# Second layer's modulations: all products on VectorE, and three of them made in the second layer itself

## The chip, the cores and the metric

The kernel runs on one core of one Trainium2 chip, as one launch. The metric is the device time of one execution in microseconds, the median of the runs; lower is better.

## The reference

Two layers of a hybrid backbone work on 128 context tokens and 512 latent tokens of width 1024, everything in fp32. Each layer has a mixing part (latent attention A, differential attention B, a Mamba-2 state-space part C, called SSD here, and one output projection) and a feed-forward part of width 4096. What the change touches are the modulations: six vectors per layer and per token group, made from the conditioning vector by one large weight matrix.

```python
mod = jax.nn.silu(c) @ w_ada[l] + b_ada[l]          # (6 * 1024); once for c_ctx, once for c
shift1, scale1, gate1, shift2, scale2, gate2 = jnp.split(mod, 6, axis=-1)
h = rmsnorm(x, p['norm1_g']) * (1.0 + scale1) + shift1
x = x + gate1 * mixing(h)
h = rmsnorm(x, p['norm2_g']) * (1.0 + scale2) + shift2
x = x + gate2 * (jnp.square(jax.nn.relu(h @ p['w_ff1'])) @ p['w_ff2'])
```

Modulation (l, j) below is vector j of layer l: j = 0 shift1, 1 scale1, 2 gate1, 3 shift2, 4 scale2, 5 gate2.

## The kernel before

All 640 tokens lie on the free axis, the features on the 128 partitions, in eight tiles. A matrix product takes each operand as two parts, a rounded one and the remainder, and adds three products of them on TensorE. ScalarE makes the rounded part of a weight tile (`wh`, line 1804 in the feed-forward part, line 296 in the mixing part) and VectorE subtracts it (`wl`, lines 1805 and 297). Weights come in 256 KB pieces over SyncE's DMA queue.

A layer runs as `mixing` and then `feed_forward`. `mixing` makes projections and SSD side by side, then attention B, then attention A, then the rest of the output projection (`wo`). `feed_forward` has four quarters q. In each, eight f1 units make 1024 hidden features (quarter 0 plainly, 1 to 3 in pairs, `ffx`, `ffy`, `ffz`), and eight f2 units multiply them by w_ff2 (`fm<-uh,wh`, line 1834). VectorE's `residual` (line 565) multiplies an f2 unit's result by the gate and adds it to `x`; until then the unit's PSUM tile is not free. The next layer's first norm is begun in the last quarter's f2 units.

The order on each engine comes from a scheduler, which takes the instructions as the code emits them. Work that has no fixed place is emitted in steps: a `Part` wraps a generator, and `weave` steps the part that is least far on by its own count. `pace(n)` sets the count of `fill`, the part of the modulations: n steps are spread over the part that is woven with it, and .01 means none. `FILL` holds the three values for projections with SSD, for the end of SSD, and for attention A.

Of the twelve modulations, (0,1) and (0,0) are made on TensorE at the start, (0,2), (0,3), (0,4) by `ada_dve` in the first layer's mixing part (the first by the end of SSD there, two in attention A), and the seven others by `ada_rows` in the first layer's feed-forward part. `ada_rows` spreads the two conditioning vectors over all partitions by 32 products with the identity (line 463, tiles `crow`), and then takes one step per 128 features: two DMAs of 256 KB (`wa`, line 470), and four products of 512 columns with their sum, one for each half of the inputs and each token group. `ROWS_POOL` says which two of the four go to GpSimd (a product at line 481, summed by ScalarE at line 482); the other two are one VectorE instruction each, product and sum (line 484). Eight steps make one modulation. In quarter 0 each f1 unit takes one step; each f2 unit takes two, save the first four of quarter 0.

The profile calls TensorE PE, VectorE DVE, ScalarE ACT, GpSimd POOL, SyncE SP.

Of the kernel before, what the change touches and what calls it, by code (L numbers as in the profile page):

```python
# [99 lines left out]
ADA_T = [(0, 5)] + [(1, j) for j in (1, 0, 2, 3, 4, 5)]  # L100
# [4 lines left out]
def build(nc, tc, a, ctx):  # L105
# [8 lines left out]
    def mark(s):  # L114
        if MARK:
            MARK(nc, s)
# [69 lines left out]
    def weave(need, *more):  # L186

        parts = list(need) + list(more)
        while any(p.live for p in need):
            e = min((p for p in parts if p.live), key=lambda p: (p.k + 0.5) / p.n)  # L190
            e.step()
# [255 lines left out]
    def ada_all(items):  # L447
        for l, j in items:
            for _ in ada_dve(l, j):
                mark("fill")  # L450
                yield
                mark("fill")

    def ada_rows(items):
# [19 lines left out]
        for i, (l, j, m, h) in enumerate(units):  # L474
            if m == 0 and h == 0:
                res = S([P, 2, KD, 2], "adares", 2)
            for v in range(2):
                junk = X([P, 512], name="junk")
                sum_ = res[:, h, m, v:v + 1]
                if 2 * h + v in ROWS_POOL:  # L480
                    pool.tensor_tensor(out=junk, in0=raws[i], in1=row[v][h], op=ALU.mult)  # L481
# [115 lines left out]
    def mixing(l, nrm, fill, late=None, raws={}):  # L597
# [1074 lines left out]
        def pace(n):  # L1672

            fill.k, fill.n = 0, n

        pace(FILL[0])
        ps_ssd, ps_proj = Part(ssd(), N_SSD, A_SSD), Part(projections(), N_PROJ)
        weave([ps_proj], ps_ssd, fill)
        p_b, p_pa = Part(att_b(), N_ATTB, A_ATTB), Part(prep_a(), N_PREP, A_PREP)
# [1 line left out]
        p_stack = Part(stack(), N_STACK, A_STACK)  # L1681
        while (0, 0, 2) not in stacks:
            p_stack.step()
        pace(FILL[1])
        weave([ps_ssd], p_b, p_pa, p_stack, fill)
        while l == 0 and fill.k < 9:
            fill.step()
# [3 lines left out]
        weave([p_b, p_pa, p_c], p_stack, fill)  # L1691
        p_s = Part(sub_all(sub_norm), N_SUB, A_SUB)
        p_a, p_w = Part(att_a(), N_ATTA, A_ATTA), Part(wo_part("wob", 4, range(2, 4), mixh, mixl, xsave, False), N_WO1)
        pace(FILL[2])
        weave([p_s], p_a, fill)
        weave([p_a, p_w], fill)
        while fill.live:
# [3 lines left out]
        for h in range(2):  # L1701
            for mi in range(4):
                mark(f"{l}wo")
                m = 4 * h + mi
# [17 lines left out]
    AHEAD = 1  # L1722
    FETCHED, AHEADS = 7, 2
    AP1, AP0 = (1, 4), ()
    FILL = (.01,6,25)
    ROWS_POOL = (1, 2)
    ADA_DVE = ((1, 4, 7), (1, 4, 7))
    CONV_POOL = ()
    ON_POOL = {f"xbc{j}" for j in range(2, 6)} | {"dv0", "dv1"}
# [144 lines left out]
    def feed_forward(l, nrm, fill):  # L1874
# [77 lines left out]
        for q in range(4):  # L1952
            uh, ul = [None] * 8, [None] * 8
            if q == 0:
                early(uh, ul)

                for m in range(8):
                    mark(f"{l}ff")
                    if m >= 2:
                        plain(m, uh, ul)  # L1960
                    fill.step()
            else:
                for m in range(4):
                    mark(f"{l}ff")
                    pair((m, m + 4), uh, ul)
                load_x(xsave, 0)
            for m in range(8):
                mark(f"{l}ff")
                if q and m + 1 < KD:
                    load_x(xsave, m + 1)  # L1970
                if q == 0 and m < 4:
                    next(expand)
                ps = PA("fm")
                for h in range(2):
                    block(halves(ps), W.next(), uh[4 * h:4 * h + 4], ul[4 * h:4 * h + 4], h == 0, h == 1)
                residual(l, 5, m, ps)
                nc.sync.dma_start(a["yT"][:, m] if l == DEPTH - 1 and q == 3 else xsave[:, m], x[m])
                if q == 3:
                    if l + 1 < DEPTH:
                        mark(f"{l + 1}norm1")  # L1980
                        nxt.scaled(l + 1, 0, m)
                        nxt.square(m)
                for _ in range(0 if q == 0 and m < 4 else 2):
                    fill.step()
        while fill.live:
            fill.step()
# [42 lines left out]
        act.copy(out=masksr[:, 0:4, :], in_=mk)  # L2029
        act.activation(out=never, in_=mk[:, M_SF:M_SB + 1], func=AF.Copy, scale=-1e30)  # L2030
    for l in range(DEPTH):
        f0 = Part(ada_all([(0, 2), (0, 3), (0, 4)]) if l == 0 else iter(()), 1)
        n2 = mixing(l, nrm, f0, *((second, raws0) if l == 0 else ()))
        f1 = Part(ada_rows(ADA_T) if l == 0 else iter(()), 57)
        nrm = feed_forward(l, n2, f1)


# [121 lines left out]
```

## Time and profile before

| | us |
|---|---|
| median of 3 runs | 1902.16 |
| lowest and highest of them | 1901.58, 1907.16 |
| the profiled execution | 1898.2 |
| its span, first to last instruction | 1896.4 |

The profile is of one execution, 4.0 us under the median of the runs and 1.8 us longer than its own span. Busy time counts work and leaves out waiting and issuing. In a row of a stretch each engine has its busy time in that stretch and the number of its instructions, then come the clock that TensorE was granted (1.00 is the upper of its two levels, 2.4 GHz, 0.50 the lower), the share of the DMA engines' time and GB/s. In a row of a group stand busy time and mean length in ns, then the idle time just before them and what ended it.

### The profile page before, as it was taken

How to read it: one execution, taken by the hardware profiler on the slowest of the kernel's cores; microseconds unless marked ns; L12 is line 12 of the kernel's file. 1: busy time of each engine (PE TensorE's matmuls, PEld its weight loads, DVE VectorE, ACT ScalarE, POOL GpSimd, SP SyncE). 2: the span in 40 equal slices, each digit the busy share in tenths (PEclk: the TensorE clock that was granted, in tenths of full speed). 3: DMA queues.
4: the chain of work that ended last, by engine and by line, in shares of the span. 5: the costliest groups of instructions: out<-in, count | busy, mean ns of one | idle time of the engine just before them, and what ended most of it. 6: DMA issues, size and time to landing. Idle time of an engine off the chain costs nothing. (4 is left out here: it accounts for less than half of the span.)

```text
span 1896.4 us, 31841 instructions
## 1 busy us (share of the span) xinstructions
PE 1735.2 (92%) x11508; PEld 1628.9 (86%) x11508; DVE 1432.1 (76%) x2587; ACT 915.3 (48%) x2009; POOL 797.5 (42%) x778
## 2 busy tenths in 40 slices
PE   6899985999898797997998899979998999999999
PEld 4798864888898797997998888768998999999999
DVE  7776778877979989889986775778746597565572
ACT  5543355665556454353555443266654454333240
POOL 4344345442546838648555443354303063130400
PEclk8899976989999999999999899879999999999999
DMA  9121123234253436456364221012121233534441
GB/s 333 48 84 41 48 61 99 66 122 137 84 167 116 135 125 213 163 188 210 99 203 132 59 63 54 23 53 77 62 73 45 73 115 93 165 109 141 126 150 57
DMA packets 116590, 209.02 MB, mean 110 GB/s; under 512 B 13392, under 2 KB 28624, under 8 KB 116432
## 3 DMA queue, kind: packets, MB, share of 16 engines
q1 hardware_dynamic: 115872, 206.80, 34.0%
q8 instruction: 91, 1.49, 0.3%
q14 instruction: 67, 0.55, 0.1%
q10 hardware_dynamic: 560, 0.18, 0.0%
HBM read 179.51 MB, written 27.43 MB: 109 GB/s over the span
## 5 line engine op out<-in xcount | busy, mean ns | idle before, releaser
L1834 PE MATMUL fm<-uh,wh 128*128 128x320 f32 x1024 | 239.2, 315 | 42.5 <-DVE x L565 42.5
L1804 ACT CAST wh<-wr 128x512 fp32r<-128x512 f32 x232 | 143.0, 617 | 221.2 <-PE fm L1834 134.0
L1805 DVE TENSOR_TENSOR wl<-wr,wh 128x512 fp32r<-128x512 f32 x232 | 204.0, 890 | 55.7 <-issue 38.9
L1834 PE MATMUL fm<-ul,wh 128*128 128x320 f32 x1024 | 238.6, 315 | 5.6 <-DVE ul L307 5.6
L481 POOL TENSOR_TENSOR junk<-wa,crow 128x512 f32<-128x512 f32 x112 | 186.9, 1689 | 126.1 <-DVE ul L307 31.9
L1834 PE MATMUL fm<-uh,wl 128*128 128x320 f32 x1024 | 237.2, 313 | 0.0
L1834 PEld LDWEIGHTS fm<-uh,wh 128*128 128x128 f32 x1024 | 174.6, 192 | 46.4 <-issue 31.9
L1834 PEld LDWEIGHTS fm<-ul,wh 128*128 128x128 f32 x1024 | 175.4, 192 | 7.2 <-DVE ul L307 7.2
L1834 PEld LDWEIGHTS fm<-uh,wl 128*128 128x128 f32 x1024 | 175.2, 192 | 0.0
L1791 POOL TENSOR_TENSOR wS<-wr,wr 128x512 f32<-128x512 f32 x48 | 76.4, 1591 | 168.3 <-DMA wr<-in_W 145.7
L484 DVE SCALAR_TENSOR_TENSOR junk<-wa,crow 128x512 f32<-128x512 f32 x112 | 139.1, 1271 | 9.0 <-DMA wa<-in_w_adaT 9.0
L565 DVE SCALAR_TENSOR_TENSOR x<-fm,mod,x 128x128 f32<-128x128 f32 (+2 forms) x192 | 72.3, 430 | 79.3 <-PE fm L1834 79.3
L785 PE MATMUL tm<-wl,hhi 128*128 128x256 f32 (+2 forms) x400 | 120.6, 302 | 4.2 <-POOL wl L297 4.2
L784 PE MATMUL tm<-wh,hhi 128*128 128x256 f32 (+2 forms) x400 | 121.5, 304 | 0.5 <-ACT xpad L628 0.5
L786 PE MATMUL tm<-wh,hlo 128*128 128x256 f32 (+2 forms) x400 | 120.3, 301 | 0.0
L482 ACT ACTIVATE junk<-junk 128x512 f32<-128x512 f32 x112 | 70.3, 628 | 89.2 <-POOL junk L481 89.2
L1804 ACT CAST wh<-wS 128x512 fp32r<-128x512 f32 x96 | 59.4, 621 | 108.0 <-PE fm L1834 37.3
L296 ACT CAST wh<-wr 128x512 fp32r<-128x512 f32 (+2 forms) x108 | 66.3, 624 | 72.8 <-PE fm L318 41.5
L1834 PE MATMUL ffx<-eh,wh 128*128 128x320 f32 x288 | 89.5, 311 | 3.1 <-ACT v L1935 3.0
L1834 PE MATMUL ffx<-eh,wl 128*128 128x320 f32 x288 | 88.8, 308 | 0.0
L1834 PE MATMUL ffx<-el,wh 128*128 128x320 f32 x288 | 88.8, 308 | 0.0
L785 PEld LDWEIGHTS tm<-wl,hhi 128*128 128x128 f32 x400 | 81.2, 203 | 5.0 <-POOL wl L297 4.5
(396 smaller groups left out, 5180.9 us busy)
## 6 DMA issues: line engine op xcount, KB each, us to landing
wr<-in_W SPq DMA_DIRECT2D x351, 256.0 KB, 2.8
wa<-in_w_adaT SPq DMA_DIRECT2D x112, 256.0 KB, 4.4
xsave<-x SPq DMA_DIRECT2D x72, 320.0 KB, 2.3
x<-xsave SPq DMA_DIRECT2D x72, 320.0 KB, 4.6
wa<-in_w_ada SPq DMA_DIRECT2D x48, 256.0 KB, 3.4
war<-in_w_ada SPq DMA_DIRECT2D x32, 256.0 KB, 5.5
x<-in_xT SPq DMA_DIRECT2D x16, 320.0 KB, 4.7
out_yT<-x SPq DMA_DIRECT2D x8, 320.0 KB, 2.2
```

The source lines that it names most:

```text
L296: act.copy(out=hi[:, :w], in_=raw[:, :w])
L481: pool.tensor_tensor(out=junk, in0=raws[i], in1=row[v][h], op=ALU.mult)
L482: act.activation(out=junk, in_=junk, func=AF.Copy, accum_out=sum_)
L484: vec.scalar_tensor_tensor(out=junk, in0=raws[i], scalar=1.0, in1=row[v][h], op0=ALU.mult, op1=ALU.mult, accum_out=sum_)
L565: vec.scalar_tensor_tensor(out=x[m][:, t0:t0 + n], in0=src, scalar=mods[l][:, j, m, v:v + 1], in1=x[m][:, t0:t0 + n], op0=ALU.mult, op1=AL ...
L784: pe.matmul(ps[:, i, :n], hh[k][:, ts], hi[:, c:c + n], start=s, stop=False)
L785: pe.matmul(ps[:, i, :n], hh[k][:, ts], lo[:, c:c + n], start=False, stop=False)
L786: pe.matmul(ps[:, i, :n], hl[k][:, ts], hi[:, c:c + n], start=False, stop=e)
L1791: pool.tensor_tensor(out=box[key], in0=box[x0], in1=box[x1], op=op)
L1804: act.copy(out=hi, in_=raw)
L1805: vec.tensor_tensor(out=lo, in0=raw, in1=f(hi), op=ALU.subtract)
L1834: mm = pe.matmul(o, w_, x_[:, ts], start=s_, stop=e_, skip_group_check=on)
```

## The change

Three things change. `ROWS_POOL` is empty, so that all four products of a step are VectorE's. The seven modulations of `ada_rows` are made in three places: (0,5), (1,1), (1,0), (1,2) in the first layer's feed-forward part, (1,3) and (1,4) in the second layer's mixing part, (1,5) in its feed-forward part; each place spreads the conditioning vectors anew. And an f2 unit takes one step instead of two, with `FILL` given per layer: for the second, 8 steps beside the projections and 9 beside attention A.

```diff
-        pace(FILL[0])
+        fills = FILL[l]
+        pace(fills[0])
...
-        pace(FILL[1])
+        pace(fills[1])
...
-        pace(FILL[2])
+        pace(fills[2])
...
-    FILL = (.01,6,25)
-    ROWS_POOL = (1, 2)
+    FILL = (.01, 6, 25), (8, .01, 9)
+    ROWS_POOL = ()
...
-                for _ in range(0 if q == 0 and m < 4 else 2):
+                if q or m >= 4:
                     fill.step()
...
-        f0 = Part(ada_all([(0, 2), (0, 3), (0, 4)]) if l == 0 else iter(()), 1)
+        f0 = Part(ada_all([(0, 2), (0, 3), (0, 4)]) if l == 0 else ada_rows([(1, 3), (1, 4)]), 1)
         n2 = mixing(l, nrm, f0, *((second, raws0) if l == 0 else ()))
-        f1 = Part(ada_rows(ADA_T) if l == 0 else iter(()), 57)
+        f1 = Part(ada_rows([(0, 5), (1, 1), (1, 0), (1, 2)] if l == 0 else [(1, 5)]), 57)
```

After the edit the lines from the first of these on stand one lower (line 1805 is 1806).

VectorE's order in the f2 units of quarter 1 of the first layer's feed-forward part, before (`junk` is a product that is summed, `x` the residual):

```order
L484 SCALAR_TENSOR_TENSOR junk_8157,adares_8051<-wa_8078,crow_6026 128x512
L484 SCALAR_TENSOR_TENSOR junk_8161,adares_8051<-wa_8152,crow_6023 128x512
L565 SCALAR_TENSOR_TENSOR x_7982<-fm_7986,mod_86,x_7982 128x128
L565 SCALAR_TENSOR_TENSOR x_7982<-fm_7986,mod_86,x_7982 128x192
L565 SCALAR_TENSOR_TENSOR x_7982<-fm_7986,mod_86,x_7982 128x320
L1805 TENSOR_TENSOR wl_8211<-wr_8113,wh_8210 128x512
L484 SCALAR_TENSOR_TENSOR junk_8171,adares_8051<-wa_8159,crow_6026 128x512
L484 SCALAR_TENSOR_TENSOR junk_8242,adares_8051<-wa_8166,crow_6023 128x512
L484 SCALAR_TENSOR_TENSOR junk_8252,adares_8051<-wa_8173,crow_6026 128x512
L484 SCALAR_TENSOR_TENSOR junk_8256,adares_8051<-wa_8247,crow_6023 128x512
L1805 TENSOR_TENSOR wl_8276<-wr_8178,wh_8275 128x512
```

Between the residuals of two f2 units stand four products and two remainders `wl`; the two `crow` tiles 6023 and 6026 are VectorE's. The same place after the change:

```order
L484 SCALAR_TENSOR_TENSOR junk_8127,adares_7042<-wa_8050,crow_6025 128x512
L484 SCALAR_TENSOR_TENSOR junk_8131,adares_7042<-wa_8056,crow_6024 128x512
L484 SCALAR_TENSOR_TENSOR junk_8133,adares_7042<-wa_8056,crow_6026 128x512
L484 SCALAR_TENSOR_TENSOR junk_8204,adares_7042<-wa_8129,crow_6023 128x512
L484 SCALAR_TENSOR_TENSOR junk_8206,adares_7042<-wa_8129,crow_6025 128x512
L565 SCALAR_TENSOR_TENSOR x_7898<-fm_7902,mod_86,x_7898 128x128
L565 SCALAR_TENSOR_TENSOR x_7898<-fm_7902,mod_86,x_7898 128x192
L565 SCALAR_TENSOR_TENSOR x_7898<-fm_7902,mod_86,x_7898 128x320
L1806 TENSOR_TENSOR wl_8094<-wr_8012,wh_8093 128x512
L484 SCALAR_TENSOR_TENSOR junk_8210,adares_7042<-wa_8135,crow_6024 128x512
L484 SCALAR_TENSOR_TENSOR junk_8212,adares_7042<-wa_8135,crow_6026 128x512
L484 SCALAR_TENSOR_TENSOR junk_8288,adares_8287<-wa_8208,crow_6023 128x512
```

Four products stand between one residual and the next in both; what is new is that the four `crow` tiles (6023 to 6026) are all VectorE's, and that an f2 unit makes one step, not two.

GpSimd's order at the same place before:

```order
L481 TENSOR_TENSOR junk_8054<-wa_7371,crow_6025 128x512
L481 TENSOR_TENSOR junk_8059<-wa_7378,crow_6024 128x512
L481 TENSOR_TENSOR junk_8068<-wa_8057,crow_6025 128x512
L481 TENSOR_TENSOR junk_8073<-wa_8064,crow_6024 128x512
L481 TENSOR_TENSOR junk_8149<-wa_8071,crow_6025 128x512
L481 TENSOR_TENSOR junk_8154<-wa_8078,crow_6024 128x512
L481 TENSOR_TENSOR junk_8163<-wa_8152,crow_6025 128x512
```

After the change no product is left on GpSimd; in these units it has nothing but the sums of weights `wS` for the pairs that come next.

VectorE's order in the second layer's mixing part, in the projections of dk, before (`dxn`, `dxr`, `dtmp` belong to the projections, `eg`, `xtm` to SSD):

```order
L758 TENSOR_TENSOR dxr_13017<-dxn_13007,tabs_11871 128x256 x2
L766 TENSOR_TENSOR dtmp_13018<-dxn_13007,tabs_11871 128x16x8 x2
L1183 TENSOR_TENSOR eg_13034<-eg_13034,dt_12257 128x512
L767 TENSOR_TENSOR dxr_13017<-dxr_13017,dtmp_13018 128x256
L1203 TENSOR_TENSOR xtm_12296<-yd_12971,xD_13068 128x512
L1185 TENSOR_TENSOR eg_13028<-eg_13028,eg_13034 128x512
L1186 TENSOR_TENSOR eg_13028<-eg_13028,cbm_12976 128x512
L297 TENSOR_TENSOR wl_13240<-wr_13237,wh_13239 128x512
L880 TENSOR_REDUCE ss_2863_13099<-dsq_13097 128x16
```

Nothing but projections, SSD and remainders of weights stands here. The same place after the change:

```order
L1186 TENSOR_TENSOR eg_12540<-eg_12540,cbm_12507 128x512
L881 TENSOR_SCALAR ss_2730_12665<-ss_2730_12665 128x16
L1183 TENSOR_TENSOR eg_12577<-eg_12577,dt_11842 128x512
L883 TENSOR_TENSOR dxn_12661<-dxn_12661,r_2731_12668 128x512
L758 TENSOR_TENSOR dxr_12671<-dxn_12661,tabs_11456 128x256 x2
L766 TENSOR_TENSOR dtmp_12672<-dxn_12661,tabs_11456 128x16x8 x2
L1185 TENSOR_TENSOR eg_12571<-eg_12571,eg_12577 128x512
L484 SCALAR_TENSOR_TENSOR junk_12693,adares_12024<-wa_12555,crow_11992 128x512
L484 SCALAR_TENSOR_TENSOR junk_12695,adares_12024<-wa_12555,crow_11994 128x512
L484 SCALAR_TENSOR_TENSOR junk_12699,adares_12024<-wa_12561,crow_11993 128x512
L484 SCALAR_TENSOR_TENSOR junk_12701,adares_12024<-wa_12561,crow_11995 128x512
L1183 TENSOR_TENSOR eg_12688<-eg_12688,dt_11842 128x512
```

The four products of a step stand between two instructions of SSD (`eg`). Nine such steps (36 products) lie beside the projections and SSD, seven (28) in attention A, eight (32) in the second layer's first f1 units, and 128 in the first layer's feed-forward part, 32 of them in its first f1 units.

## Rows read from the trace of the kernel before

**Rows 1.** The page: span, and busy time, share and instructions of each engine.
```profile
span 1896.4 us, 31841 instructions
...
PE 1735.2 (92%) x11508; PEld 1628.9 (86%) x11508; DVE 1432.1 (76%) x2587; ACT 915.3 (48%) x2009; POOL 797.5 (42%) x778
```

**Rows 2.** Stretches by engine: first layer's feed-forward (two), second layer's mixing and feed-forward.
```profile
core 0: us, PE busy (x) PEld busy (x) DVE busy (x) ACT busy (x) POOL busy (x), PEclk, DMA share, GB/s
513.40:578.60 65.20, 64.27 (x439) 63.33 (x438) 55.10 (x84) 40.07 (x94) 34.41 (x30) 1.00 0.46 147
578.60:1019.90 441.30, 389.43 (x2543) 382.50 (x2543) 408.26 (x589) 216.76 (x475) 283.35 (x183) 0.97 0.50 163
1020.20:1453.00 432.80, 397.97 (x2688) 357.03 (x2686) 303.30 (x664) 219.06 (x500) 165.30 (x217) 0.93 0.19 58
1453.00:1515.10 62.10, 61.52 (x406) 61.29 (x407) 33.71 (x46) 25.88 (x51) 4.92 (x3) 0.97 0.24 69
1515.10:1892.00 376.90, 374.94 (x2544) 374.07 (x2543) 230.59 (x356) 138.20 (x251) 90.78 (x64) 1.00 0.37 119
```

**Rows 3.** Waits of PE, 578.6 to 1019.9: who for whom, us, times, longest.
```profile
engine line waited for: us in total, times, longest us
PE fm L1834 <- DVE x L565: 40.5, 16, 6.9
PE fm L1834 <- DVE ul L307: 5.6, 6, 2.2
```

**Rows 4.** Waits of PE, 1515.1 to 1892, all of them.
```profile
PE fm L1834 <- DVE x L565: 2.0, 1, 2.0
```

**Rows 5.** Groups of DVE, 578.6 to 1019.9.
```profile
line engine op names shapes xcount | busy us, mean ns | idle before us <-releasers
L484 DVE SCALAR_TENSOR_TENSOR junk<-wa,crow 128x512 f32<-128x512 f32 x98 | 126.8, 1322 | 9.0 <-DMA wa<-in_w_adaT 9.0
L1805 DVE TENSOR_TENSOR wl<-wr,wh 128x512 fp32r<-128x512 f32 x96 | 96.4, 1019 | 4.9 <-issue 3.9 <-PE ffy L1834 1.1
...
L565 DVE SCALAR_TENSOR_TENSOR x<-fm,mod,x 128x128 f32<-128x128 f32 (+2 forms) x93 | 34.9, 427 | 2.5 <-PE fm L1834 2.5
...
L307 DVE TENSOR_TENSOR ul<-u,uh 128x640 fp32r<-128x640 f32 x26 | 28.7, 1105 | 0.5
```

**Rows 6.** Groups of DVE, 1515.1 to 1892.
```profile
L1805 DVE TENSOR_TENSOR wl<-wr,wh 128x512 fp32r<-128x512 f32 x96 | 71.6, 753 | 44.8 <-issue 32.5 <-PE ffy L1834 8.5 <-ACT wh L1804 2.2
...
L307 DVE TENSOR_TENSOR ul<-u,uh 128x640 fp32r<-128x640 f32 x25 | 21.5, 862 | 0.6
```

**Rows 7.** Timeline of DVE from 642: start us, us, instruction.
```profile
644.77 1.80 DVE L484 SCALAR_TENSOR_TENSOR junk<-wa,crow 128x512 f32<-128x512 f32 x1
...
646.50 0.68 DVE L484 SCALAR_TENSOR_TENSOR junk<-wa,crow 128x512 f32<-128x512 f32 x1
...
647.11 1.77 DVE L484 SCALAR_TENSOR_TENSOR junk<-wa,crow 128x512 f32<-128x512 f32 x1
```

**Rows 8.** Timeline of POOL, same stretch.
```profile
642.50 3.52 POOL L481 TENSOR_TENSOR junk<-wa,crow 128x512 f32<-128x512 f32 x2 [0.50 <-DMA wa<-in_w_adaT]
646.65 5.09 POOL L481 TENSOR_TENSOR junk<-wa,crow 128x512 f32<-128x512 f32 x3 [0.64 <-DVE junk L484]
```

**Rows 9.** Stretches as in rows 2: projections and SSD, then attention A, second layer.
```profile
1117.00:1210.00 93.00, 91.78 (x542) 73.31 (x542) 60.35 (x122) 35.26 (x86) 39.69 (x34) 0.93 0.18 53
1353.00:1449.00 96.00, 92.38 (x744) 90.33 (x744) 55.31 (x114) 51.76 (x113) 17.16 (x22) 1.00 0.17 55
```

**Rows 10.** The same, attention A of the first layer.
```profile
393.00:513.40 120.40, 109.53 (x812) 105.64 (x813) 92.83 (x197) 68.57 (x163) 45.02 (x46) 0.93 0.38 120
```

**Rows 11.** The products that spread the conditioning vectors: ns min/median/max, first and last start.
```profile
L463 PE MATMUL crow<-identr,sc x32: 270/275/275, 531.9 to 537.4; 128*128 128x128 f32 x32
```

**Rows 12.** The products, and the remainders of weights, on VectorE: ns min/median/max.
```profile
L484 DVE SCALAR_TENSOR_TENSOR junk<-wa,crow x112: 676/1747/1818, 542.1 to 1004.3; 128x512 f32<-128x512 f32 x112
L1805 DVE TENSOR_TENSOR wl<-wr,wh x232: 673/692/2012, 497.8 to 1874.5; 128x512 fp32r<-128x512 f32 x116
```

## The prediction, made before the changed kernel was run

> **What bounds the kernel now.** I read the page first. TensorE is busy for 92% of the span and VectorE for 76% [rows 1], so on average this is a TensorE kernel; but both layers do the same feed-forward work, and the average hides how they differ. So next I cut the span into stages [rows 2]. From the first f2 unit to the last, the second layer takes 376.9 us with TensorE busy for 374.9 of them. The first layer takes 441.3 us for the same products: TensorE is busy for 389.4, and VectorE for 408.3, 93% of the stretch. That is 64.4 us more, and the only work the first layer has on top is the modulations and the next layer's norm.
>
> Then the waits. In the second layer TensorE waits 2.0 us in that stretch [rows 4]. In the first it waits 40.5 us for residuals and 5.6 us for the remainder `ul` [rows 3], both VectorE's: an f2 unit cannot start because VectorE is late in emptying an earlier one's tile.
>
> Why VectorE is so late stands in its groups [rows 5]. The 98 products cost 126.8 us, 1322 ns each. Yet the shortest of the 112 takes 676 ns and the median 1747 [rows 12]: the instruction has two prices. The timeline tells them apart [rows 7, 8]. The product at 644.77 runs while GpSimd is in a product of its own and takes 1.80 us. The one at 646.50 starts in the gap of GpSimd that ends at 646.65 and takes 0.68; the next, at 647.11, falls into GpSimd's following run and takes 1.77. Other VectorE work with two inputs in SBUF pays too: 96 remainders `wl` take 1019 ns each here and 753 in the second layer, `ul` 1105 and 862 [rows 5, 6]. So the modulations cost VectorE twice, by its own products and by GpSimd's, which slow everything next to them.
>
> **The change, part by part.**
>
> *First layer, f2 units and pairs.* VectorE keeps its number of products in this stretch: 24 steps of four, 96, for 48 steps of two. What goes is GpSimd's share (and ScalarE's sums of it, which nobody on TensorE's path waits for). Per f2 unit with fill, VectorE has now three residuals (3 x 0.427), two remainders (2 x 1.019) and four products (4 x 1.322), 8.6 us [rows 5], against 48 products of TensorE at 376.9 / 2544 = 0.148 us, 7.1 us [rows 2]. So VectorE falls behind by 1.5 us in each of 24 units, 36 us; the rest of the 64 I put down to slower remainders elsewhere and to the lower clock (0.97 for 1.00). Without GpSimd the same unit has 1.28 + 2 x 0.753 + 4 x 0.68 = 5.5 us, and TensorE is the bound. For the whole stretch: VectorE's 230.6 us of the second layer, plus 96 products at 0.94 (GpSimd stays busy for 90.8 of 376.9 us there, a share of 0.24, with weight sums: 0.76 x 0.68 + 0.24 x 1.77), 90 us, plus some 20 us for norm and finishing, is 341 of 377. I leave 5 us for the norm in the last quarter and take 382 us: **-59**. Bounds: -64 if it becomes the second layer's; -20 if every product still costs 1.77 (170 + 231 + 20 = 421 us of VectorE, and the stretch as long as that).
>
> *First layer, f1 units.* 32 products replace 16, but 16 of GpSimd's go; VectorE is at 55.1 of 65.2 us with GpSimd busy for 34.4, and TensorE at 64.3 [rows 2]. **0**, between -1 and +5.
>
> *Spreading the vectors again, twice.* 32 small products on TensorE, started over 5.5 us among others [rows 11]; the first layer's f1 stretch, which has them, is 65.2 against 62.1 us [rows 2]. **+3** in each place (0 to 5.5).
>
> *Second layer, projections and SSD.* 36 products. TensorE is busy for 91.8 of 93 us, VectorE for 60.4, GpSimd for 39.7, a share of 0.43 [rows 9]. At 0.57 x 0.68 + 0.43 x 1.77 = 1.15 us they are 41 us, and VectorE has 33 idle. They also stand in the queue ahead of SSD's `eg`, which TensorE will want. Most is covered by the projections, which need little of VectorE; what is not covered shows at the end of SSD. I take **+12**, between 0 (all in idle time) and +41 (all on the path), nearer the first, since TensorE has no idle time to give there. The 16 steps' DMAs, two of 256 KB each, join SyncE's queue among the weights; the DMA engines are busy for 0.18 of this stretch, so I cost them at nothing; without that cover a weight would come later by a step's two transfers.
>
> *Second layer, attention A.* 28 products. VectorE is busy for 55.3 of 96 us, GpSimd for 17.2, a share of 0.18 [rows 9]: 28 x (0.82 x 0.68 + 0.18 x 1.77) = 25 us into 41 idle. But softmax chains run through VectorE. The first layer makes two modulations in this same stage and takes 120.4 us [rows 10], 12.2 more per modulation, with TensorE work and GpSimd sums that the new form does not have. 28 products are 7/8 of a modulation: at most 10.7 by that row. **+8**, between 0 and +25.
>
> *Second layer, f1 units.* 32 products at 0.68, 22 us, into 28 idle us of VectorE (33.7 of 62.1 busy, GpSimd 4.9 [rows 2]): **0** beside the spreading, up to +8.
>
> Sum: -59 + 0 + 3 + 12 + 8 + 3 = **-33 us** against the profiled execution's 1898.2, which gives 1865. The median of the runs is 4.0 us above that execution, so 1902.2 - 33 = **1869 us**.
>
> **A rule that speaks against it.** An undisturbed product with its sum takes 0.68 us [rows 7], no more than a remainder of the same size, which makes no sum: 692 ns in the median [rows 12]. The Trainium skill, "Vector Engine (DVE) Microarchitecture Reference", section "Points that are easy to get wrong", says that this form with two fp32 inputs from SBUF runs at half throughput, since both read ports are taken. No row of this trace shows such a halving where GpSimd rests, so I give it little, as the fourth rival. By that rule an undisturbed product would be an estimated 1.38 us, twice a remainder, and the outcome that rival's.
>
> **The rivals.**
>
> 1. *The second layer hides it all* (TensorE is full there, VectorE has idle time): -59 + 3 + 3 = -53, 1849 us. Against it: SSD and softmax wait in VectorE's queue. 15%.
>
> 2. *VectorE becomes the bound of the projections: slower.* The 36 products meet SSD's own GpSimd work and cost 1.77 each, 64 us, all ahead of `eg`; attention A pays 10.7. -59 + 3 + 64 + 11 + 3 = +22, 1924 us. It decides once the second layer pays more than 59 us, that is more than 53 for 64 products, 0.83 us each on the path. For it: 41 us of products for 33 idle. Against: GpSimd is busy for only 0.43 of it [rows 9]. 4%.
>
> 3. *The first layer stays VectorE's* because the weight sums and the norm's sums on GpSimd fall on the products: -20 + 26 = +6, 1908 us, on the edge of no difference. Against: the second layer has the same weight sums and its remainders cost 753 ns [rows 6]. 5%.
>
> 4. *The products are dear in themselves*, and 1322 ns is their own price. The stretch keeps 127 us of products and loses only the slower remainders, 25 + 7 us [rows 5, 6]: 376 busy, at today's 93% 406 us, -35. The second layer's 20 us become 20 x 1322 / 1000 = 26, and its f1 units want 33.7 + 42 of 62 us, +14; the first's +5. -35 + 3 + 26 + 14 + 3 + 5 = +16, 1918 us. 2%.
>
> That the change does not do what it says is excluded by the order of the instructions: 224 products, all on VectorE.
>
> **How the numbers follow.** The forecast has 74%, the rivals 15, 4, 5 and 2. Its own terms reach from about -52 (half of each cost in the second layer) to -15 (first layer -50, projections +20, attention A +10), so the range is 1850 to 1887 us; it leaves out half of the first rival and the last three. About 0.3%, 5.7 us, is what a measurement of this kernel can tell from no change. Faster: 74 + 15, 0.89. Same: most of the third rival, 0.04. Slower: the second, the fourth and what is left of the third, 0.07.
>
> **What would show it right or wrong.** In the profile of the changed kernel the first layer's f2 stretch should last about 382 us, with VectorE near 340 and TensorE's wait for residuals under 10; products should have a mean near 0.8 us there, and `wl` near 0.75. The second layer's mixing part, 432.8 us now, should be near 456, its f1 stretch near 65. The prediction is wrong if the first layer's stretch stays above 400, or if the mixing part grows by over 40; in the latter case the wait to look for is TensorE's for `eg` or for the attention parts behind SSD.

## The result, and the profile after

The changed kernel takes 1879.2 us, the median of 4 runs (1877.8 to 1880.3), against 1901.9 for the kernel before in the same series: a ratio of 0.989, 95% interval 0.986 to 0.991. The forecast was 1869 us, range 1850 to 1887. The profiled execution takes 1878.6 us, its span is 1876.8, 19.6 below the span before [rows 1].

The page after, span and busy time by engine:

```profile
span 1876.8 us, 31813 instructions
...
PE 1744.0 (93%) x11572; PEld 1641.7 (87%) x11572; DVE 1387.1 (74%) x2811; ACT 851.1 (45%) x1793; POOL 606.2 (32%) x666
```

GpSimd lost 191 us of work and VectorE 45, though VectorE now makes twice as many products. The stages after, in the order of [rows 2]: first layer's f1 units, its f2 units and pairs, the second layer's mixing part, f1 units, f2 units and pairs.

```profile
516.50:580.40 63.90, 63.54 (x437) 63.02 (x436) 50.52 (x108) 31.44 (x64) 7.63 (x13) 1.00 0.49 153
580.40:974.00 393.60, 379.05 (x2547) 377.34 (x2546) 309.61 (x587) 154.45 (x279) 115.14 (x85) 0.99 0.46 150
974.30:1423.30 449.00, 410.45 (x2717) 367.51 (x2716) 346.89 (x796) 222.15 (x505) 166.69 (x217) 0.90 0.24 74
1423.30:1486.70 63.40, 63.40 (x437) 63.40 (x438) 47.69 (x102) 28.03 (x55) 4.50 (x3) 1.00 0.45 137
1486.70:1872.00 385.30, 378.27 (x2545) 376.84 (x2544) 230.48 (x369) 138.17 (x251) 93.95 (x64) 0.99 0.37 117
```

Against [rows 2] these are -1.3, -47.7, +16.2, +1.3 and +8.4 us, together -23.1; the first layer's mixing part, which is the same program in both, and the ends make up the other 3.5. So the first layer wins nearly 48 us and the second gives 26 back, 8 of them in its f2 units, beside which no step is emitted.

TensorE's waits in the first layer's f2 stretch after (us, times, longest), where it waited 46 us in all [rows 3]:

```profile
PE fm L1835 <- DVE x L565: 8.0, 4, 4.3
PE fm L1835 <- DVE ul L307: 6.5, 3, 3.7
```

VectorE's groups in the same stretch, those of [rows 5]:

```profile
L1806 DVE TENSOR_TENSOR wl<-wr,wh 128x512 fp32r<-128x512 f32 x96 | 75.4, 796 | 18.3 <-issue 12.2 <-PE ffy L1835 4.0 <-ACT un L1901 1.2
L484 DVE SCALAR_TENSOR_TENSOR junk<-wa,crow 128x512 f32<-128x512 f32 x101 | 73.4, 776 | 1.8 <-DMA wa<-in_w_adaT 1.7
```

The same number of products (101 for 98) costs 73.4 us instead of 126.8, and a remainder `wl` takes 796 ns instead of 1019. This is the step on which the forecast rested, and it is there as forecast.

Quarter 0's eight f2 units, first layer before, second layer before, first after, second after, as stretches of their own, each up to the first product of the pairs:

```profile
578.60:653.40 74.80, 59.73 (x385) 58.27 (x384) 74.50 (x106) 40.19 (x86) 58.05 (x37) 0.95 0.38 120
1515.10:1574.90 59.80, 57.85 (x384) 57.59 (x384) 48.78 (x72) 28.39 (x53) 34.60 (x26) 0.97 0.35 110
```
```profile
580.40:653.50 73.10, 61.40 (x385) 60.21 (x385) 63.73 (x117) 28.96 (x53) 34.97 (x24) 0.93 0.34 108
1486.70:1554.80 68.10, 61.07 (x385) 60.34 (x385) 52.09 (x85) 28.56 (x53) 40.80 (x27) 0.92 0.30 96
```

Nearly the whole 8.4 us of the second layer's f2 stretch are in its quarter 0 (68.1 for 59.8). The first layer's quarter 0 is still 13 us above 59.8, and hardly shorter than before the change (73.1 for 74.8): nearly all of the 47.7 us were won behind it. In the second layer's quarter 0 TensorE now waits 7.0 us where it waited 2.0 [rows 4], and it is busy for 3.2 us more at a granted clock of 0.92 for 0.97. Its waits in the second layer's f2 stretch after:

```profile
PE fm L1835 <- DVE ul L307: 3.7, 1, 3.7
PE fm L1835 <- DVE x L565: 3.3, 1, 3.3
```

What happens there shows at the end of the second layer's f1 units. VectorE's timeline after (start, us, instruction):

```profile
1491.07 0.82 DVE L1894 SCALAR_TENSOR_TENSOR u<-un 128x640 f32<-128x640 f32 x1
1491.81 0.69 DVE L484 SCALAR_TENSOR_TENSOR junk<-wa,crow 128x512 f32<-128x512 f32 x1
...
1493.64 0.69 DVE L484 SCALAR_TENSOR_TENSOR junk<-wa,crow 128x512 f32<-128x512 f32 x1
...
1494.26 1.94 DVE L1849 SCALAR_TENSOR_TENSOR nh<-x,amul,nR 128x128 f32<-128x128 f32 x4
1496.11 0.82 DVE L307 TENSOR_TENSOR ul<-u,uh 128x640 fp32r<-128x640 f32 x1
```

The same `ul` before the change:

```profile
1520.43 0.82 DVE L307 TENSOR_TENSOR ul<-u,uh 128x640 fp32r<-128x640 f32 x1
```

The last f1 unit's `u` is ready at 1491.9, but its remainder `ul`, which the f2 units need, stands behind four products and the first instructions (`nh`, line 1849) of the expansion, which makes from the norm's result the operands of the pairs. It ends at 1496.9, 10.2 us after the stretch began. Before the change the first `nh` stand ahead of it too, and it ends 6.2 us after the stretch began: the products make it 4 us later.

Two theories come out of this. The first: what GpSimd's products took from VectorE was the cost, and the move to the second layer was needed as well, since an f2 unit with eight products would be 1.28 + 1.5 + 8 x 0.69 = 8.3 us of VectorE for TensorE's 7.1. Its rival: GpSimd was all of it, and the move only costs. The second theory: the 8 us in the second layer's quarter 0 come from the products of (1,5) in its f1 units.

### The profile page after: what moved, and what is told of

Its sections match the earlier page's. It is cut to its first block, busy times and chain, and to the rows that moved or that the text cites. A ratio compares the mean times of both kernels' runs of the same rounds, so it can differ in the third digit from the quotient of the medians.

```text
span 1876.8 us, 31813 instructions
## 1 busy us (share of the span) xinstructions
PE 1744.0 (93%) x11572; PEld 1641.7 (87%) x11572; DVE 1387.1 (74%) x2811; ACT 851.1 (45%) x1793; POOL 606.2 (32%) x666
## 5 line engine op out<-in xcount | busy, mean ns | idle before, releaser
L1835 PE MATMUL fm<-ul,wh 128*128 128x320 f32 x1024 | 237.0, 313 | 10.2 <-DVE ul L307 10.2
L1806 DVE TENSOR_TENSOR wl<-wr,wh 128x512 fp32r<-128x512 f32 x232 | 179.7, 782 | 80.8 <-issue 48.5
L1835 PE MATMUL fm<-uh,wl 128*128 128x320 f32 x1024 | 235.9, 312 | 0.0
L1792 POOL TENSOR_TENSOR wS<-wr,wr 128x512 f32<-128x512 f32 x48 | 72.4, 1509 | 329.3 <-DMA wr<-in_W 281.5
L484 DVE SCALAR_TENSOR_TENSOR junk<-wa,crow 128x512 f32<-128x512 f32 x224 | 156.4, 747 | 5.0 <-DMA wa<-in_w_adaT 4.8
L1805 ACT CAST wh<-wS 128x512 fp32r<-128x512 f32 x96 | 59.8, 623 | 147.0 <-PE fm L1835 70.7
L784 PEld LDWEIGHTS tm<-wh,hhi 128*128 128x128 f32 x400 | 82.3, 206 | 5.2 <-DVE zth L805 2.8
L1806 DVE TENSOR_TENSOR wl<-wS,wh 128x512 fp32r<-128x512 f32 x96 | 76.8, 800 | 11.5 <-issue 11.0
```

Source lines behind the costliest of these rows:

```text
L484: vec.scalar_tensor_tensor(out=junk, in0=raws[i], scalar=1.0, in1=row[v][h], op0=ALU.mult, op1=ALU.mult, accum_out=sum_)
L784: pe.matmul(ps[:, i, :n], hh[k][:, ts], hi[:, c:c + n], start=s, stop=False)
L1792: pool.tensor_tensor(out=box[key], in0=box[x0], in1=box[x1], op=op)
L1805: act.copy(out=hi, in_=raw)
L1806: vec.tensor_tensor(out=lo, in0=raw, in1=f(hi), op=ALU.subtract)
L1835: mm = pe.matmul(o, w_, x_[:, ts], start=s_, stop=e_, skip_group_check=on)
```

## Experiments

### One half of the change each

GpSimd's products alone, from the kernel before:

```diff
-    ROWS_POOL = (1, 2)
+    ROWS_POOL = ()
```

> The kernel before, with all four products of a step on VectorE; two steps per f2 unit and all seven modulations in the first layer stay. Theory (GpSimd's products slow VectorE's two-input work, and an f2 unit is late when VectorE's work between two residuals exceeds TensorE's 7.1 us): a unit has 1.28 + 1.5 + 8 x 0.69 = 8.3 us of VectorE for 7.1, against 8.6 before, so the first layer's f2 stretch stays VectorE's and falls only from 441 to between 415 and 435 us; time 1877 to 1895. Rival A (all of the gain is from taking GpSimd off): the stretch falls to about 394 as in the changed kernel, and with nothing in the second layer the time is about 1853. Rival B (products cost 1.3 us of their own): stretch above 480, time above 1940.

The move alone, from the changed kernel:

```diff
-    ROWS_POOL = ()
+    ROWS_POOL = (1, 2)
```

> The changed kernel, with two of a step's four products on GpSimd as before. Theory (what counts is VectorE's work per f2 unit): one step leaves 1.28 + 2 x 1.0 + 2 x 1.32 = 5.9 us for TensorE's 7.1, so the first layer's f2 stretch is within 10 us of the changed kernel's 393.6, and the second layer pays some more in its mixing part (449 to 465), where GpSimd has work of its own: time 1880 to 1900. Rival (taking GpSimd off is what gave the first layer its gain): the stretch stays above 415, time above 1905.

GpSimd's products alone give 1863.4 us, ratio 0.982 (0.980 to 0.984): 16 us faster than the changed kernel. The move alone gives 1898.5, ratio 0.999 (0.996 to 1.002): nothing. First layer's f2 stretch and second layer's mixing part, of the first half alone (e1) and then of the move alone (e2):

```profile
579.50:984.80 405.30, 383.53 (x2547) 379.46 (x2547) 380.83 (x787) 153.99 (x280) 120.80 (x85) 0.98 0.55 176
985.00:1418.40 433.40, 397.93 (x2686) 358.52 (x2684) 300.99 (x664) 218.72 (x500) 167.00 (x217) 0.93 0.19 58
```
```profile
577.30:987.50 410.20, 384.67 (x2547) 381.44 (x2546) 318.71 (x485) 186.67 (x379) 196.67 (x135) 0.97 0.45 144
987.80:1442.90 455.10, 409.43 (x2717) 364.77 (x2715) 343.25 (x732) 241.02 (x569) 207.41 (x249) 0.91 0.24 73
```

The kernel before, the changed one and these two make a square. The f2 stretch is 441.3 us before, 405.3 without GpSimd's products, 410.2 with the move alone, 393.6 with both. Each half by itself brings most of the gain there, but only the move has a price in the second layer: once GpSimd is out, it buys 11.7 us in this stretch and costs 25 in the second layer. Of e1's expectations none came: the stretch lies between the theory's (415 to 435) and rival A's (394), and the time, 1863, is nearer to rival A's 1853 than to the theory's 1877; rival B is far off. The theory's error is in 0.69 us a product: that is how long its record lasts, but in the queue the next begins before the record ends, 0.61 us after the start of the one before (1491.81 to 1493.64 above is three steps). Over the stretch VectorE's 380.8 us fit into 405.3. Of e2 the theory's time (up to 1900) and mixing part came, but the stretch is 16.6 us above the changed kernel's, where 10 were allowed; the rival asked for over 415 and over 1905. So the sum of an f2 unit (5.9 us for 7.1) is not all. TensorE still waits 20.6 us for residuals in e2's stretch, 10.8 of them in quarter 0 and 9.8 early in the f2 units of quarters 1 and 2, where VectorE comes to a run of products at up to 1.77 us each.

### What GpSimd's operation does to VectorE

On the kernel of e1, useless work for GpSimd that nobody waits for: once a product that reads a `crow` tile twice, once fills (`jk` is a tile of its own).

```diff
+        jk = Y([P, 512], name="jk")
...
+            pool.tensor_tensor(out=jk, in0=row[1][h], in1=row[1][h], op=ALU.mult)
```

> The kernel of e1 (all seven modulations in the first layer, all products on VectorE), and two products on GpSimd per step whose result nobody uses: both inputs are spreading tiles in SBUF, the output is a tile of its own, no engine waits for it. GpSimd so does as much as in the kernel before (112 products of 1.69 us), while VectorE has nothing less to do. Theory (two inputs from SBUF on VectorE and a GpSimd operation that reads SBUF exclude each other): products beside them take 1.77 us again, their mean in the first layer is above 1.1 us, the f2 stretch grows from 405 to between 455 and 500 us and the time from 1863 to between 1913 and 1960. Rival (GpSimd's results, ScalarE's sums of them and the waits for them were what cost, not GpSimd's reading): stretch within 8 us of 405.

```diff
+        jk = Y([P, 512], name="jk")
...
+            for _ in range(4):
+                pool.memset(jk, 0.0)
```

> The kernel of e1, and on GpSimd four fills of a 128x512 tile in place of each useless product of e5: GpSimd is as busy to within a third or so, but reads nothing. Theory (reading is what excludes): products stay at 0.69 us, f2 stretch within 5 us of 405, time 1858 to 1868. Rival (any GpSimd operation on SBUF slows VectorE): products with a mean above 1.0 us, the stretch above 440.

With the reads 1936.8 us, ratio 1.020 (1.016 to 1.024); with the fills 1864.6, ratio 0.982 (0.978 to 0.986), the time of e1. VectorE's products and GpSimd's useless work over the whole program, reads (e5) and then fills (e6):

```profile
L485 DVE SCALAR_TENSOR_TENSOR junk<-wa,crow 128x512 f32<-128x512 f32 x224 | 205.4, 960 | 0.0
...
L487 POOL TENSOR_TENSOR jk<-crow 128x512 f32<-128x512 f32 x112 | 158.8, 1418 | 17.6 <-ACT bsh L559 9.4 <-ACT crow L464 1.4
```
```profile
L485 DVE SCALAR_TENSOR_TENSOR junk<-wa,crow 128x512 f32<-128x512 f32 x224 | 163.3, 773 | 0.0
...
L488 POOL MEMSET jk<- 128x512 f32 x448 | 235.9, 527 | 22.5
```

The fills keep GpSimd busy for longer (235.9 us for 158.8) and cost nothing: products have 773 ns, in e1 772, the first layer's f2 stretch takes 405.7 us for 405.3, and all that the theory expected came. The reads lengthen products to 960 ns. The first layer's f1 and f2 stretches with the reads:

```profile
518.10:601.60 83.50, 68.10 (x438) 66.13 (x437) 74.78 (x103) 30.40 (x64) 58.21 (x51) 0.94 0.35 108
601.60:1061.30 459.70, 395.85 (x2548) 388.70 (x2547) 442.99 (x795) 154.07 (x282) 228.26 (x162) 0.96 0.49 157
```

They are 18 and 54 us longer than e1's; 73 us for 112 GpSimd products, 0.65 us each on TensorE's path. The theory's times and its stretch came; its mean for a product (above 1.1 us) did not, since the useless products also ran beside other work of VectorE: in the f2 stretch a remainder `wl` has 904 ns with the reads and 775 with the fills. The residuals, whose one input lies in PSUM, have 425 and 426 ns. This is what the Trainium skill, "SBUF — State Buffer", section "Who interferes with whom", states: a VectorE instruction with two inputs from SBUF gets in the way of a GpSimd instruction that reads SBUF, not of one that only writes it. These two runs agree with it; a GpSimd operation with one input was not tried.

### The products left out

From the changed kernel, once without the products of the mixing part, once without those of the second layer's f1 units; their sums are set to zero (shown for the first; the second has `((1, 5),)` there):

```diff
+                skip = (l, j) in ((1, 3), (1, 4))
...
-                if 2 * h + v in ROWS_POOL:
+                if skip:
+                    pass
+                elif 2 * h + v in ROWS_POOL:
```

> The changed kernel without the 64 products of (1,3) and (1,4); their DMAs, the spreading of the vectors and the finishing stay. Theory (the products' place in VectorE's queue is what the mixing part pays): its 449.0 us fall to 433 to 437, time 1863 to 1868. Rival (spreading, DMAs on SyncE's queue and TensorE's clock are what it pays): the part stays above 443.

> The changed kernel without the 32 products of (1,5) in the second layer's f1 units; DMAs, spreading and finishing stay. Theory (these products push VectorE's work into quarter 0's first f2 units, where the expansion of the norm's result already fills it): the f2 stretch falls from 385.3 to 376 to 379 us and the f1 stretch from 63.4 to 62 to 63.4; time 1868 to 1873. Rival (the 8 us in the f2 stretch are of another origin, such as a transfer or the clock): the stretch stays above 383.

Without the mixing part's products: 1854.0 us, ratio 0.977 (0.975 to 0.980). The part takes 428.5 us, 20.5 less than with them and 4 less than before the change. So spreading the vectors and the DMAs cost nothing there that these runs can tell; the price is the products'. The part's own data don't depend on (1,3) and (1,4), which the feed-forward part uses. Both numbers are better than the theory's 433 to 437 and 1863 to 1868; how far mixing parts of nearly one program differ from run to run is told below. Without the products of (1,5): 1872.3 us, ratio 0.986 (0.983 to 0.989). The second layer's f1 and f2 stretches:

```profile
1423.70:1488.60 64.90, 64.90 (x437) 64.90 (x438) 33.39 (x48) 27.51 (x55) 4.48 (x3) 0.97 0.43 134
1488.60:1865.80 377.20, 375.33 (x2545) 374.43 (x2544) 228.50 (x356) 138.21 (x251) 91.36 (x64) 1.00 0.38 119
```

The f2 stretch is back at 377.2 us, as before the change (376.9): the second theory holds, its rival falls. The f1 stretch is 2.8 us above that of before, which leaves the spreading; its expectation (62 to 63.4) did not come.

How the mixing part pays shows in its 30 us slices at the end of SSD, at the same distance from the part's start. Changed kernel, then the one without the products:

```profile
1154.00:1184.00 30.00, 27.60 (x137) 21.26 (x136) 23.82 (x47) 7.37 (x20) 6.95 (x6) 0.73 0.24 71
1184.00:1214.00 30.00, 23.20 (x110) 18.89 (x109) 25.97 (x63) 10.89 (x25) 6.11 (x8) 0.67 0.20 63
1214.00:1244.00 30.00, 24.36 (x104) 17.96 (x104) 21.51 (x61) 21.93 (x55) 16.76 (x39) 0.69 0.18 55
```
```profile
1150.00:1180.00 30.00, 29.86 (x161) 24.01 (x160) 24.72 (x47) 8.24 (x20) 7.42 (x7) 0.79 0.30 89
1180.00:1210.00 30.00, 22.16 (x134) 19.15 (x133) 20.47 (x58) 20.89 (x50) 10.77 (x26) 0.89 0.20 60
1210.00:1240.00 30.00, 25.33 (x156) 21.09 (x157) 25.16 (x69) 22.08 (x57) 19.39 (x31) 0.89 0.16 54
```

With the products TensorE does 351 matmuls in 90 us, without them 451, at a granted clock of 0.67 to 0.73 instead of 0.79 to 0.89. Over the whole part TensorE is idle for 5.6 us more (38.5 for 32.9) and busy for 14.9 more, at a clock of 0.90 for 0.94: three quarters of the 20.5 us are TensorE's own work, more of it at the lower level. The fall of the clock goes with the waits; that they cause it was not tried by itself. Which of VectorE's results came late first is not settled; the trace names only single waits there.

### Better places

On e1, quarter 0's expansion in f2 units 0, 2, 4, 6, no steps in that quarter's f2 units. In both kernels the expansions from the second on read x after a residual has been added, so their values differ, not their instructions.

```diff
-                if q == 0 and m < 4:
+                if q == 0 and m % 2 == 0:
                     next(expand)
...
-                for _ in range(0 if q == 0 and m < 4 else 2):
+                for _ in range(2 if q else 0):
```

> The kernel of e1, with the expansion of the norm's result put into quarter 0's f2 units 0, 2, 4, 6 instead of 0, 1, 2, 3, in both layers, and no steps in quarter 0's f2 units (the others take two each, which makes the same 56 steps). Theory (quarter 0 is late because VectorE has f1's backlog, the expansion and steps at once): quarter 0's eight units take some 65 us in the first layer for 79, and 58 for 61 in the second; f2 stretches 390 to 399 and 372 to 376, time 1848 to 1858. Rival (VectorE is full over the whole stretch, 381 of 405 us, so that what quarter 0 saves comes back in quarter 3, which now has eight more steps): first layer's stretch above 402, time 1858 to 1865.

Then also a step beside each pair (the loop above becomes `range(1 + m % 2 if q else 0)`):

```diff
                     pair((m, m + 4), uh, ul)
+                    fill.step()
```

> As e7, but a step beside each of the 12 pairs of f1 units, and one and two in turn beside the f2 units of quarters 1 to 3 (36 there). Theory (an f2 unit with two steps has 3 x 0.36 + 10 x 0.61 = 7.2 us in VectorE's queue for TensorE's 7.05, so it falls behind by a little in each; pairs leave VectorE idle for a fifth): the first layer's stretch is 3 to 8 us below e7's. Rival (in the pairs VectorE's sums of TensorE's results are on the path, and GpSimd's weight sums make the products dear there): the stretch is longer than e7's.

Both missed the time. e7 takes 1865.5 us, ratio 0.982 (0.980 to 0.985), no better than e1. In the first layer its theory came: quarter 0's f2 units take 65.1 us (72.4 in e1) and the f2 stretch 397.0; in the second the f2 stretch is 376.9. But the second layer's mixing part, whose code is e1's, takes 441.6 for 433.4. It starts with VectorE still behind from the steps in quarter 3: 24 products run in its first 27 us, in e1 none, and TensorE's sums for its norm (`nss`) begin 20.2 us into the part, in e1 7.5. The rival comes nearest in time and in its reason, but what quarter 0 saves comes back one stage later than it said. e8 takes 1878.7 us, ratio 0.988 (0.985 to 0.992), with an f2 stretch of 413.3, longer than e7's as its rival had it. TensorE's longest group of waits there (e8):

```profile
PE ffx L1834 <- ACT v L1935: 14.4, 6, 2.4
```

In a pair TensorE goes on writing into the same tile `ffx`; it cannot until ScalarE has copied that into a `v`. Ahead of these copies ScalarE is idle in turn, six times for 1.01 us, until a product of VectorE ends. The first such product and its copy (e8):

```profile
663.68 1.75 DVE L484 SCALAR_TENSOR_TENSOR junk<-wa,crow 128x512 f32<-128x512 f32 x1
```
```profile
665.53 0.43 ACT L1935 COPY v<-ffx 128x320 f32<-128x320 f32 x1 [1.01 <-DVE junk L484]
```

The product runs beside a weight sum of GpSimd (663.15 to 664.88) and takes 1.75 us; TensorE goes on at 666.00, after 2.40 us of waiting. This is the rival's second reason: products are dear beside the weight sums, and here one is on TensorE's path. In the code `junk` and `v` are tiles of one pool of buffers (`X`), which would explain why a copy waits for a product; that was not tried by itself. VectorE's idle fifth in the pairs is not free time.

Next, six modulations in the first layer and one, (1,4), in the second layer's mixing part, beside attention A (e9, shown) or, with `(9, .01, .01)`, beside the projections (e10):

```diff
-    FILL = (.01, 6, 25), (8, .01, 9)
+    FILL = (.01, 6, 25), (.01, .01, 9)
...
-                if q or m >= 4:
+                for _ in range(2 if q else 0):
...
-        f0 = Part(ada_all([(0, 2), (0, 3), (0, 4)]) if l == 0 else ada_rows([(1, 3), (1, 4)]), 1)
+        f0 = Part(ada_all([(0, 2), (0, 3), (0, 4)]) if l == 0 else ada_rows([(1, 4)]), 1)
...
-        f1 = Part(ada_rows([(0, 5), (1, 1), (1, 0), (1, 2)] if l == 0 else [(1, 5)]), 57)
+        f1 = Part(ada_rows([(0, 5), (1, 1), (1, 0), (1, 2), (1, 3), (1, 5)]) if l == 0 else iter(()), 57)
```

> As e1, with six modulations in the first layer and one, (1,4), in the second layer's mixing part, all of it beside attention A; no steps in quarter 0's f2 units, two in the others until they are used up (48 steps in the first layer). Theory (the mixing part pays where VectorE's queue holds SSD's chains at the end of the projections, not beside attention A): the mixing part is 434 to 441 us for e1's 433.6, the first layer's f2 stretch 394 to 400 for 405.3, time 1856 to 1864. Rival (any place in the mixing part costs about as much, 8 us or more a modulation): mixing part above 441, time above 1864.

> As e9, with (1,4) beside the projections and SSD instead of attention A. Theory: most of what the changed kernel's mixing part pays is here and goes with the clock that falls after the late SSD chains: mixing part 442 to 450 us, time 1864 to 1874, longer than e9 by 5 to 12. Rival (same price in either place): within 3 us of e9.

They take 1863.2 us, ratio 0.978 (0.975 to 0.982), and 1862.5, ratio 0.980 (0.975 to 0.984). Of e9 all that its theory expected came; of e10 the mixing part (441.5 us) came to within 1 us, the time not. By the time e10's rival is right: the place makes no difference that can be measured. First layer's f2 stretch, then the mixing part in two pieces, to the end of the projections' matmuls and from there on; e9, then e10:

```profile
590.00:984.60 394.60, 379.13 (x2547) 376.08 (x2547) 356.61 (x720) 154.00 (x280) 118.89 (x85) 0.99 0.53 172
984.70:1202.80 218.10, 206.84 (x1322) 181.73 (x1320) 151.87 (x291) 89.23 (x205) 90.61 (x105) 0.93 0.19 54
1202.80:1419.70 216.90, 194.26 (x1399) 177.15 (x1397) 169.95 (x440) 132.12 (x300) 76.42 (x112) 0.95 0.25 81
```
```profile
579.70:973.90 394.20, 378.99 (x2547) 375.93 (x2547) 355.91 (x720) 153.92 (x280) 119.41 (x85) 0.99 0.53 173
974.00:1206.40 232.40, 214.32 (x1354) 188.82 (x1352) 174.01 (x362) 91.82 (x207) 90.35 (x105) 0.91 0.23 68
1206.40:1415.50 209.10, 189.12 (x1367) 173.15 (x1366) 149.76 (x371) 129.29 (x298) 73.49 (x112) 0.95 0.21 66
```

The same pieces of e1, which has no modulation there, and of the changed kernel:

```profile
985.00:1206.20 221.20, 208.12 (x1321) 183.81 (x1319) 149.01 (x291) 89.13 (x205) 91.17 (x105) 0.92 0.19 53
1206.20:1418.40 212.20, 189.81 (x1367) 174.71 (x1365) 151.97 (x375) 129.58 (x296) 75.83 (x112) 0.94 0.20 64
```
```profile
974.30:1209.00 234.70, 217.91 (x1353) 190.93 (x1351) 176.71 (x364) 91.50 (x207) 92.39 (x105) 0.88 0.23 70
1209.00:1423.30 214.30, 192.55 (x1366) 176.58 (x1366) 170.18 (x433) 130.65 (x299) 74.29 (x112) 0.92 0.25 78
```

One modulation beside the projections costs 11 us in its piece, one beside attention A about 5. But in e9 the projections, with nothing new in them, happened to take 218.1, and in e11 below, which has the same edit in the mixing part, 224.1. A single profile tells prices of this size to 3 us at best, and e9's mixing part at 435.0, as expected, is in part chance.

What this pair does show is the first layer: it makes six modulations in 394 us, the time in which the changed kernel makes four, and the seventh (e1) brings it to 405.

Last, the eight steps of quarter 0's f1 units put into the first six of them, on e9 and on the changed kernel:

```diff
-                    fill.step()
+                    for _ in range((2, 2, 1, 1, 1, 1, 0, 0)[m]):
+                        fill.step()
```

> The kernel of e9, with the eight steps of quarter 0's f1 units in the first six of them: two each after the first two units, one each after the next four, none after the last two. Theory (products that stand ahead of the last f1 units' remainders are what puts quarter 0's f2 units late): the first layer's f2 stretch falls from 394.6 to between 386 and 391 us, its f1 stretch stays within 2 us of 65.1, and the time is 4 to 8 us below e9's. Rival (quarter 0 is late from the sum of VectorE's work there, wherever the products stand): f2 stretch above 392.5.

> The changed kernel with the same edit, which acts in both layers. Theory: f2 stretches 393.6 to 386 to 390 us and 385.3 to 377 to 380 us, time 1863 to 1870. Rival: f2 stretches within 2 us of the changed kernel's, time 1876 to 1882.

e11 takes 1865.0 us, ratio 0.981 (0.979 to 0.983): no gain on e9. e12 takes 1873.4, ratio 0.985 (0.983 to 0.987), some 6 us below the changed kernel, with intervals that still touch. Its f1 and f2 stretches, first layer and second:

```profile
524.60:593.80 69.20, 65.85 (x438) 64.66 (x437) 55.45 (x122) 31.90 (x66) 10.06 (x16) 0.98 0.47 145
593.80:979.30 385.50, 376.62 (x2548) 375.14 (x2547) 307.20 (x575) 154.39 (x279) 112.27 (x85) 1.00 0.48 153
...
1429.60:1495.50 65.90, 63.56 (x436) 63.30 (x437) 51.18 (x114) 27.66 (x55) 4.48 (x3) 1.00 0.44 132
1495.50:1873.60 378.10, 375.52 (x2546) 374.50 (x2544) 228.24 (x357) 138.49 (x251) 90.33 (x64) 1.00 0.37 119
```

The f2 stretches fall by 8.1 and 7.2 us, as the theory has it: the place of the products ahead of the last `ul` matters, in both layers. But the f1 stretches grow by 5.3 and 2.5, which goes with the rival's reason, the sum of VectorE's work: it is then late inside them. The time misses the theory's 1863 to 1870. In e11 the f2 stretch falls to 391.4, between the two expectations, and the f1 stretch takes 69.2 for 65.1, so that nothing is left.

Four versions stand at 1862 to 1865 us: e1, e9, e10 and e11. They are not told apart by these runs, and all beat both kernels. The simplest is the kernel before with `ROWS_POOL` empty.

## Why the prediction was right, and where it was not

The time lies 10 us above the point, within the range and on the side that had 0.89. That it lies no further off is partly luck: by stages the forecast misses by +11 us in the first layer's f2 units and pairs, -1 in its f1 units, -7 in the mixing part and +7 in the second layer's f1 and f2 units together. The lower end of the range does not follow from its terms either: -59 with half of each cost in the second layer is -46, not -52. By its own steps:

- **First layer, f2 units and pairs, -59: the mechanism right, the size off.** It came to -47.7 (393.6 us for 382). VectorE's busy time is 309.6 us, where about 340 was allowed; products have 776 ns and `wl` 796, where 0.8 and 0.75 us were said. What was left out is the start of the stretch: of the 16.7 us that it takes beyond the second layer's 376.9, quarter 0 has 13.3 (73.1 us for 59.8). The step gave 5 us for the norm in the last quarter, where nothing was lost (its f2 units take 56.6 us from 917.4 on, in the second layer before 56.5), and nothing for the first.
- **First layer, f1 units, 0**: -1.3.
- **Spreading, +3 each**: in f1 units +1.3 with the products and +2.8 without them (e4), in the mixing part nothing that can be told (e3).
- **Projections and SSD, +12**: 234.7 us to the end of the projections' matmuls for 221.7, +13.0. The size is in part luck: a product was priced at 1.15 us, and the 36 have 817 ns. The same cut at 1241.9 in the trace before:

```profile
1020.20:1241.90 221.70, 209.96 (x1324) 184.05 (x1322) 149.74 (x291) 89.60 (x205) 89.87 (x105) 0.92 0.18 52
1241.90:1453.00 211.10, 188.00 (x1366) 172.97 (x1364) 153.57 (x375) 129.47 (x296) 75.42 (x112) 0.95 0.20 64
```

- **Attention A, +8**: the second piece went from 211.1 to 214.3, +3.2. With the spreading's 3 the mixing part was to pay 23 and paid 16.2.
- **Second layer, f1 units, "0 beside the spreading, up to +8": the step that failed.** It cost 8.4 us, at the upper end, and one stage later. The cover named was 28 idle us of VectorE in the f1 stretch; those are spread over it, while the last products stand ahead of the last `ul` and run into the expansion. Idle time was counted over the stretch instead of read at its end. Without the products the cost is gone (e4).
- **What the sum could not show.** It priced the change as a whole, and its two halves never separately. It put the first layer's gain down to GpSimd's leaving, while the move by itself brings 31 of the 48 us there (e2). The rows of the products' two prices [rows 7, 8] were already an argument that GpSimd's part alone might do; e1 shows that it does, with 16 us to spare.

Rival 1 (the second layer hides all) fell by 26 us; so did rival 3, with the first layer's gain, and rival 4: undisturbed products run in 0.69 us, beside remainders without a sum at 0.69 (VectorE's timeline, 1478 to 1491 us: lines 484 and 1806). The halving that the Trainium skill's "Vector Engine (DVE) Microarchitecture Reference", "Points that are easy to get wrong", states for this form is not seen in any run here. Rival 2 (VectorE bound in the projections) asked for 1.77 us a product and +64; with 817 ns the piece grew by 13.

## What to carry to other kernels

When one instruction has two prices in a trace, look for what runs beside the dear ones before moving work: taking the disturber away was worth 37 us and moving the work nothing. Idle time of an engine covers new work only if it lies where that work stands in the queue; read it at the end of a stage, where the next stage waits, not as the stage's sum. And price the halves of a change apart, since one can be paid for by the other.

## What was not expected of the hardware

- Fills on GpSimd, 236 us of them, leave VectorE's two-input work as it is, and 159 us of products that read SBUF cost 73 us of the program's time.
- A product's record lasts 0.69 us, but in a row of products one starts every 0.61 us, each with a 0.08 us read of its sum beside the next.
- In the mixing part 5.6 us of added waits came with 14.9 us more of busy time for the same number of matmuls (granted clock 0.90 for 0.94): more of the cost came as a lower clock than as waits.
- The same instructions do not take the same time from run to run: the first layer's f1 stretch begins at 513.4 us in one profile and at 524.6 in e12's, with the same work before it. Stages were therefore compared each with its own start.
